# Probabilities times values in a latent attention: the stationary tile takes the values of two heads (128 columns) instead of one (64)

## The chip, the cores and the metric

The kernel runs on one core of one Trainium2 chip. Times are device microseconds of one execution. A profile of one execution shows the five engines: TensorE (PE its matmuls, PEld its weight loads), VectorE (DVE), ScalarE (ACT), GpSimd (POOL) and SyncE (SP, which issues the transfers here).

## The reference, cut to what matters

One step of a network with two layers, for 128 context tokens and 128 latent tokens. Each layer is a feed-forward part, a token mixer and another feed-forward part, with a normalisation behind each. The mixer has three branches: a convolution, a retention and an attention with low-rank queries and keys. The change is in the attention, in the product of probabilities and values:

```python
kv = (ckv_all @ lp['mla_w_ukv']).reshape(B, ckv_all.shape[1], MLA_HEADS, MLA_D_NOPE + MLA_D_V)
s = jnp.einsum('bqhd,bkhd->bhqk', qn, k_nope) + jnp.einsum('bqhd,bkd->bhqk', qr, k_rope)
p = jax.nn.softmax(s.astype(jnp.float32) * scale, axis=-1).astype(v.dtype)
out = jnp.einsum('bhqk,bkhd->bqhd', p, v)
mla_out = attn.reshape(B, T, MLA_HEADS * MLA_D_V) @ lp['mla_w_out']
```

There are 8 heads with 64 value columns each. A context token sees the 128 context keys; a latent token sees 128 cached keys and the 128 latent keys. So a head has three blocks of 128 x 128 probabilities.

## The kernel before, in words

Activations lie with features on partitions and the 256 tokens (128 context, 128 latent) along the free axis. The weights arrive as 458 units of up to 128 x 1024 values in the order in which they are used. ScalarE rounds a unit to a short format (`ring_hi`, line 692) and VectorE makes the rest (`ring_lo`, line 693), both in rings of five; a projection is then three matmuls per block of 128 features: high by high, high by low, low by high. The matmuls of a unit in the main chain are 24 for most projections; units with 512 moving columns have 12 or 18.

All instructions are first recorded in a `Program`. Its `order` (line 350) plays them through with modelled durations and due times, engine by engine, and each engine's instructions are then written in that order, which is fixed from then on. Main matmuls form one chain; side work (attention, retention, convolution taps, modulation products) is given slots with `sched` and is laid between the matmuls of the chain. The model of a matmul (`matmul`, line 454) depends on its moving columns, not on its stationary ones. A bank of the matmul memory counts as a whole when dependences are found (`region`, line 285). A side matmul on TensorE is ready only some time after what it needs (`PAD`, line 249).

The attention of a head has three steps. `att0` makes scores and probabilities: query times key, the maximum, the exponential with its sum, and the division. `att1` transposes the three blocks of probabilities on TensorE into bank C, and ScalarE copies them to `pt` (`ring_aa`). `att2` multiplies: the stationary operand is a block of values of this head, 128 keys x 64 columns out of `vm` (tile T6, shown as T in the profile), the moving operand the transposed probabilities of 128 tokens. The operands have 32-bit floats, and each such matmul leaves two loads and two matmuls in the trace. Even heads write partitions 0 to 63 of bank E and odd heads partitions 64 to 127, in the same 256 columns. After the odd head ScalarE copies the pair, rounded, into `catm` (tile CM), and VectorE subtracts that from the bank to make the low part; these are lines 1412 to 1415, recorded at lines 520 and 482. `catm` is read by the units `("mla", p)`, the first of which starts some 60 us after the last of these copies.

Of the kernel before, what the change touches and what calls it, by code (L numbers as in the profile page):

```python
# [8 lines left out]
F32 = mybir.dt.float32  # L9
# [3 lines left out]
AF = mybir.ActivationFunctionType  # L13
ALU = mybir.AluOpType
PSUM = bass.MemoryType.PSUM

P = 128
# [5 lines left out]
T = 256  # L23
# [541 lines left out]
class Trunk:  # L565
# [632 lines left out]
    def mixer(self, l):  # L1198
# [43 lines left out]
        for j in range(2):  # L1242
            ps = self.bank("C" if j == 0 else "B")
# [53 lines left out]
        ps = self.bank()  # L1297
# [29 lines left out]
        st = {}  # L1327
# [9 lines left out]
        for j in range(4):  # L1337
            ps = self.bank()
# [18 lines left out]
        vm = self.t("T6", [3, 512])  # L1357
# [14 lines left out]
        catm = self.t("CM", [4, 2, T], F32R)  # L1372
# [27 lines left out]

        def att2(h):
            pt = st.pop(("t", h))
            o = (h % 2) * 64
            if h % 2 == 0:
                st["o"] = self.bank("E")
            po = st["o"][o:o + 64]
            v = lambda b: vm[:, b, h * 64:(h + 1) * 64]
            nc.matmul(po[:, 0:TOK], v(0), pt[:, 0:TOK], start=True, stop=True)
            nc.matmul(po[:, TOK:T], v(1), pt[:, TOK:2 * TOK], start=True, stop=False)
            nc.matmul(po[:, TOK:T], v(2), pt[:, 2 * TOK:3 * TOK], start=False, stop=True)  # L1410
            if h % 2:
                ps = st["o"][:, 0:T]
                c = catm[:, h // 2, 0, :]
                self.act(c, ps, AF.Copy)
                self.tt(catm[:, h // 2, 1, :], ps, c.bitcast(F32), ALU.subtract)

        for h in range(MH):
            self.sched(h + 4, lambda h=h: att2(h))
# [291 lines left out]
        for f in range(KT):  # L1710
            ps = self.bank()
# [118 lines left out]
```

## Time and profile before

| what | value |
|---|---|
| time, median of 3 runs | 1413.1 us (1409.68 to 1414.0) |
| the profiled execution's own time | 1410.63 us |
| its span in the profile | 1408.9 us |
| PE busy | 1374.7 us (98%) |
| DVE busy | 1206.7 us (86%) |
| ACT busy | 765.8 us (54%) |
| read from the chip's memory | 321.28 MB, 230 GB/s over the span |
| mean granted TensorE clock | 0.995 of full speed |

How to read the rows below: a group row has the line, engine, operation, output<-inputs and shape, the count, the busy time and mean duration in ns of one, and the idle time of the engine just before them with what ended it. A matmul's `128*64` is the part of the array that it uses, rows by columns. The durations of matmuls overlap, since they are pipelined; what one costs is read from the start of one to the start of the next.

### The profile page before, as it was taken

How to read it: one execution, taken by the hardware profiler on the slowest of the kernel's cores; microseconds unless marked ns; L12 is line 12 of the kernel's file. 1: busy time of each engine (PE TensorE's matmuls, PEld its weight loads, DVE VectorE, ACT ScalarE, POOL GpSimd, SP SyncE). 2: the span in 40 equal slices, each digit the busy share in tenths (PEclk: the TensorE clock that was granted, in tenths of full speed). 3: DMA queues.
4: the chain of work that ended last, by engine and by line, in shares of the span. 5: the costliest groups of instructions: out<-in, count | busy, mean ns of one | idle time of the engine just before them, and what ended most of it. 6: DMA issues, size and time to landing. Idle time of an engine off the chain costs nothing.

```text
span 1408.9 us, 28827 instructions
## 1 busy us (share of the span) xinstructions
PE 1374.7 (98%) x11488; PEld 1309.0 (93%) x11488; DVE 1206.7 (86%) x2291; ACT 765.8 (54%) x1257; POOL 13.6 (1%) x28
## 2 busy tenths in 40 slices
PE   7999999999999999999999999999999999999996
PEld 5999998987999999999989999899788999899996
DVE  3899988998999988999989999799889998865565
ACT  4654447565554557444465454675555455754542
POOL 0000000000000000000000000000000000000000
PEclk9999999999999999999999999999999999999998
DMA  9998975753567767889658896655346767466561
GB/s 349 349 325 286 333 263 205 239 168 123 173 215 261 233 243 269 280 288 337 238 192 301 283 311 236 228 186 165 119 139 211 246 222 264 140 223 196 181 194 57
DMA packets 92166, 326.60 MB, mean 232 GB/s; under 512 B 10944, under 2 KB 11360, under 8 KB 91392
## 3 DMA queue, kind: packets, MB, share of 16 engines
q1 hardware_dynamic: 90432, 319.88, 66.5%
q0 software_dynamic: 1600, 4.88, 1.0%
q8 instruction: 90, 1.47, 0.4%
q14 instruction: 44, 0.36, 0.1%
HBM read 321.28 MB, written 3.44 MB: 230 GB/s over the span
## 4 chain that ended last, share of the span: by engine, by line
PE 91%; DVE 5%; DMA 3%; ACT 1%; issue 1%; SPq 0%; DVEq 0%; ACTq 0%
PE bankm L460 66%; PE bankE L460 18%; PE bankB L460 2%; PE bankA L460 2%; PE bankC L460 2%; DVE ring_lo L482 2%; DVE T L486 1%; DMA T<-in_ada 1%; DVE T L482 1%; DMA T<-in_x 1%; DMA ring_ada<-in_ada 0%; DMA ring_raw<-in_w 0%; PE bankC L473 0%; ACT ring_hi L520 0%; SPq L527 0%
## 5 line engine op out<-in xcount | busy, mean ns | idle before, releaser
L520 ACT ACTIVATE ring_hi<-ring_raw 128x1024 fp32r<-128x1024 f32 (+2 forms) x462 | 476.8, 1037 | 327.5 <-PE bankm L460 143.4
L482 DVE TENSOR_TENSOR ring_lo<-ring_raw,ring_hi 128x1024 fp32r<-128x1024 f32 (+2 forms) x462 | 546.0, 1192 | 81.7 <-ACT ring_hi L520 79.9
L460 PE MATMUL bankm<-ring_U,ring_hi 128*128 128x256 f32 x3296 | 588.4, 280 | 5.7 <-ACT ring_U L520 2.8
L460 PEld LDWEIGHTS bankm<-ring_U,ring_hi 128*128 128x128 f32 x3296 | 503.4, 189 | 12.4 <-ACT ring_U L520 3.7
L460 PE MATMUL bankm<-ring_U,ring_lo 128*128 128x256 f32 x1648 | 463.9, 281 | 0.2
L460 PEld LDWEIGHTS bankm<-ring_U,ring_lo 128*128 128x128 f32 x1648 | 310.8, 189 | 4.0 <-issue 2.3
L460 PE MATMUL bankm<-T,ring_hi 128*128 128x256 f32 x1464 | 255.1, 277 | 2.3 <-DVE T L482 2.3
L460 PEld LDWEIGHTS bankm<-T,ring_hi 128*128 128x128 f32 x1464 | 221.1, 188 | 3.4 <-ACT ring_hi L520 3.0
L460 PE MATMUL bankm<-T,ring_lo 128*128 128x256 f32 (+1 forms) x732 | 202.9, 277 | 0.0
L460 PE MATMUL bankE<-ring_U,ring_hi 128*128 128x256 f32 x832 | 146.8, 277 | 0.0
L460 PEld LDWEIGHTS bankm<-T,ring_lo 128*128 128x128 f32 x732 | 137.4, 188 | 0.0
L460 PEld LDWEIGHTS bankE<-ring_U,ring_hi 128*128 128x128 f32 x832 | 125.8, 188 | 0.4 <-issue 0.4
L486 DVE SCALAR_TENSOR_TENSOR T<-hp,cols,T 128x256 f32<-128x256 f32 x240 | 114.1, 481 | 3.8
L460 PE MATMUL bankE<-ring_U,ring_lo 128*128 128x256 f32 x416 | 115.3, 277 | 0.1
L460 PE MATMUL bankm<-ring_hi,ring_U 128*128 128x512 f32 x256 | 88.6, 414 | 0.0
L520 ACT ACTIVATE ring_tB<-bankm 128x256 f32<-128x256 f32 x84 | 31.7, 382 | 102.6 <-PE bankm L460 102.5
L460 PE MATMUL bankE<-T,ring_hi 128*128 128x256 f32 (+1 forms) x488 | 86.5, 279 | 0.0
L460 PEld LDWEIGHTS bankE<-ring_U,ring_lo 128*128 128x128 f32 x416 | 78.4, 188 | 0.3 <-DVE ring_lo L482 0.3
L486 DVE SCALAR_TENSOR_TENSOR ring_s<-ring_ada,ring_sg 128x1024 bf16<-128x1024 f32 (+2 forms) x68 | 74.3, 1093 | 2.5 <-DMA ring_ada<-in_ada 2.4
L460 PEld LDWEIGHTS bankE<-T,ring_hi 128*128 128x128 f32 x488 | 74.1, 188 | 1.0 <-DVE T L482 0.8
L486 DVE SCALAR_TENSOR_TENSOR ring_ada<-ring_ada,ring_sg 128x1024 f32<-128x1024 f32 (+2 forms) x68 | 73.8, 1092 | 0.1
L460 PE MATMUL bankE<-T,ring_lo 128*128 128x256 f32 (+1 forms) x244 | 68.1, 279 | 0.0
(263 smaller groups left out, 1594.0 us busy)
## 6 DMA issues: line engine op xcount, KB each, us to landing
ring_raw<-in_w SPq DMA_DIRECT2D x422, 512.0 KB, 4.4
ring_ada<-in_ada SPq DMA_DIRECT2D x107, 512.0 KB, 5.2
ring_raw<-in_w SPq DMA_DIRECT2D x32, 384.0 KB, 4.0
T<-in_ada SPq DMA_DIRECT2D x17, 512.0 KB, 7.7
ring_aa<-in_ada SPq DMA_DIRECT2D x10, 512.0 KB, 6.6
CM<-in_ada SPq DMA_DIRECT2D x6, 512.0 KB, 6.9
ring_sg<-in_crow SPq DMA_DIRECT2D x3, 1024.0 KB, 5.8
ring_raw<-in_w SPq DMA_DIRECT2D x8, 256.0 KB, 7.5
```

Of the source, the lines that this page charges most:

```text
L460: self.prog.add("PE", dur, lambda: self.nc.tensor.matmul(self.real(out), self.real(lhsT), self.real(rhs), start=start, stop=stop), [lhsT, ...
L482: self.dve(out, [in0, in1], lambda: self.nc.vector.tensor_tensor(out=self.real(out), in0=self.real(in0), in1=self.real(in1), op=op))
L486: self.dve(out, [in0, scalar, in1], lambda: self.nc.vector.scalar_tensor_tensor(out=self.real(out), in0=self.real(in0), scalar=self.real(s ...
L520: self.prog.add("ACT", dur, lambda: self.nc.scalar.activation(self.real(out), self.real(in_), func, **{k: self.real(v) for k, v in kw.item ...
```

## The change

The stationary operand becomes the values of both heads of a pair, 128 columns. Each head writes all 128 partitions, into its own half of bank E (columns 0 to 255 for the even head, 256 to 511 for the odd one). Of the even head's half only partitions 0 to 63 are of use, of the odd head's half partitions 64 to 127; the other rows are the products with the other head's values and are not read. The copy and the subtraction behind the odd head are made once for each half, on 64 partitions each.

```diff
         def att2(h):
             pt = st.pop(("t", h))
-            o = (h % 2) * 64
-            if h % 2 == 0:
+            e, pair = h % 2, h // 2
+            if e == 0:
                 st["o"] = self.bank("E")
-            po = st["o"][o:o + 64]
-            v = lambda b: vm[:, b, h * 64:(h + 1) * 64]
+            po = st["o"][:, e * T:(e + 1) * T]
+            v = lambda b: vm[:, b, pair * P:(pair + 1) * P]
             nc.matmul(po[:, 0:TOK], v(0), pt[:, 0:TOK], start=True, stop=True)
             nc.matmul(po[:, TOK:T], v(1), pt[:, TOK:2 * TOK], start=True, stop=False)
             nc.matmul(po[:, TOK:T], v(2), pt[:, 2 * TOK:3 * TOK], start=False, stop=True)
-            if h % 2:
-                ps = st["o"][:, 0:T]
-                c = catm[:, h // 2, 0, :]
-                self.act(c, ps, AF.Copy)
-                self.tt(catm[:, h // 2, 1, :], ps, c.bitcast(F32), ALU.subtract)
+            if e:
+                for a in range(2):
+                    rows = slice(a * 64, a * 64 + 64)
+                    ps = st["o"][rows, a * T:(a + 1) * T]
+                    c = catm[rows, pair, 0, :]
+                    self.act(c, ps, AF.Copy)
+                    self.tt(catm[rows, pair, 1, :], ps, c.bitcast(F32), ALU.subtract)
```

## Rows read from the trace of the kernel before

**Rows 1.** The page: busy us and share per engine; the last chain by engine.
```profile
PE 1374.7 (98%) x11488; PEld 1309.0 (93%) x11488; DVE 1206.7 (86%) x2291; ACT 765.8 (54%) x1257; POOL 13.6 (1%) x28
...
PE 91%; DVE 5%; DMA 3%; ACT 1%; issue 1%; SPq 0%; DVEq 0%; ACTq 0%
```

**Rows 2.** Groups of weight loads by form, whole span.
```profile
L460 PEld LDWEIGHTS bankE<-ring_aa,T 128*64 128x64 f32 x96 | 9.2, 134 | 12.0 <-issue 9.0 <-DVE ring_mx L502 0.7 <-DVE T L486 0.5
...
L460 PEld LDWEIGHTS bankA<-T 128*128 128x128 f32 x32 | 5.3, 189 | 0.3
```

**Rows 3.** Timeline of TensorE's matmuls: start us, us, engine, line, what, count.
```profile
307.90 0.63 PE L460 MATMUL bankm<-ring_hi,ring_U 128*128 128x512 f32 x2
308.45 0.43 PE L460 MATMUL bankE<-ring_aa,T 128*64 128x128 f32 x2
308.82 0.50 PE L460 MATMUL bankm<-ring_lo,ring_U 128*128 128x512 f32 x1
309.16 0.63 PE L460 MATMUL bankm<-ring_hi,ring_U 128*128 128x512 f32 x2
309.63 0.38 PE L460 MATMUL bankA<-T,T 128*128 128x128 f32 x2
309.84 0.27 PE L473 MATMUL bankC<-const,ring_aa 128*128 128x128 f32 x1
310.05 0.43 PE L460 MATMUL bankE<-ring_aa,T 128*64 128x128 f32 x2
310.41 0.50 PE L460 MATMUL bankm<-ring_lo,ring_U 128*128 128x512 f32 x1
310.74 0.63 PE L460 MATMUL bankm<-ring_hi,ring_U 128*128 128x512 f32 x2
...
311.44 0.27 PE L473 MATMUL bankC<-const,ring_aa 128*128 128x128 f32 x1
311.55 0.60 PE L460 MATMUL bankA<-T,T 128*128 128x256 f32 x2
...
314.05 0.43 PE L460 MATMUL bankE<-ring_aa,T 128*64 128x128 f32 x2
```

**Rows 4.** Timeline of the weight loads, same stretch; idle before and its end in brackets.
```profile
308.45 0.19 PEld L460 LDWEIGHTS bankE<-ring_aa,T 128*64 128x64 f32 x2 [0.36 <-issue]
308.82 0.19 PEld L460 LDWEIGHTS bankm<-ring_lo,ring_U 128*128 128x128 f32 x1 [0.17 <-issue]
...
309.40 0.42 PEld L460 LDWEIGHTS bankA<-T,T 128*128 128x128 f32 x2
```

**Rows 5.** Instructions of bank E: count, ns min/median/max, first and last start.
```profile
L520 ACT ACTIVATE CM<-bankE x8: 367/378/385, 310.9 to 1030.9; 128x256 fp32r<-128x256 f32 x8
L482 DVE TENSOR_TENSOR CM<-bankE,CM x8: 417/424/426, 311.8 to 1031.3; 128x256 fp32r<-128x256 f32 x8
```

**Rows 6.** Groups of ScalarE by form, whole span.
```profile
L520 ACT ACTIVATE T<-bankm 64x384 f32<-64x384 f32 x6 | 2.9, 487 | 6.0 <-PE bankm L460 6.0
```

**Rows 7.** Timeline of VectorE, 310 to 315 us.
```profile
311.83 0.42 DVE L482 TENSOR_TENSOR CM<-bankE,CM 128x256 fp32r<-128x256 f32 x1
```

**Rows 8.** Timeline of TensorE's matmuls, 411 to 413.5 us.
```profile
412.50 0.40 PE L460 MATMUL bankm<-ring_U,ring_hi 128*128 128x256 f32 x2
```

**Rows 9.** Timeline of VectorE, 380 to 416 us.
```profile
408.44 1.22 DVE L482 TENSOR_TENSOR ring_lo<-ring_raw,ring_hi 128x1024 fp32r<-128x1024 f32 x1
```

**Rows 10.** Stretches: us, busy of each engine, clock, transfers' share, GB/s.
```profile
301.00:346.00 45.00, 45.00 (x246) 32.45 (x245) 37.05 (x80) 23.29 (x54) 0.00 (x0) 1.00 0.39 127
346.00:410.00 64.00, 64.00 (x396) 57.41 (x395) 58.10 (x142) 35.97 (x62) 3.81 (x7) 1.00 0.53 172
410.00:440.00 30.00, 30.00 (x266) 29.46 (x266) 29.76 (x51) 13.97 (x18) 0.00 (x0) 1.00 0.85 278
```

**Rows 11.** TensorE's waits, whole span: us in total, times, longest.
```profile
PE bankm L460 <- ACT ring_hi L520: 2.1, 1, 2.1
```

## The prediction

> **What bounds the kernel now.** I read the page's shares and its chain first. TensorE is busy 98% of the span, the chain that ended last is 91% TensorE, and VectorE is the only other engine near full [rows 1]. So a TensorE microsecond saved is worth up to one microsecond, as long as VectorE can follow.
>
> Then the changed instructions. The 96 weight loads of the probabilities-times-values matmuls (two records a matmul: 48 matmuls, 24 a layer) have 64 columns, take 134 ns, and had 12.0 us of idle weight-load time right before them; a 128-column load takes 189 ns [rows 2]. That idle time is odd in a stage where nothing is missing, so I read the order of TensorE's instructions there [rows 3]. A 512-column matmul of the main chain starts 0.235 us after the one before (309.16 to 309.63 holds two). From 307.90 to 309.16 stand three of these and one 64-column matmul: 1.26 - 3 x 0.235 = 0.555 us for it. From 309.84 to 310.74 stand a transpose (0.11, from 311.44 to 311.55), one main matmul and again one 64-column matmul: 0.90 - 0.11 - 0.235 = 0.555. The query-times-key matmul at 309.63 has the same shape but 128 stationary columns: 0.21 us to the next start. I take 0.23, with 0.02 on top for what may start late behind it; so a visit at 64 columns costs 0.33 us more than one at 128.
>
> The loads show how it arises [rows 4]: the load for 64 columns starts 0.36 us after the load engine went idle, together with its matmul, and the main load behind it 0.17 us late, each put down to "issue"; the two loads of the 128-column matmul start at 309.40, ahead of their matmuls at 309.63. So a change of the tile's width, either way, keeps the next load from running ahead.
>
> No two of these matmuls stand side by side: 1.6 us and other work lie between 308.45 and 310.05 [rows 3], and so it is for all of them.
>
> [...]
>
> **The change, part by part.**
> *Matmuls.* 48 before, 48 after, with the same moving columns and two records each; width 128 throughout. Removed 48 x 0.555, added 48 x 0.23: 26.6 - 11.0 = 15.6 us less on TensorE, 7.8 us a layer, spread over the 44 us in which they stand. Bounds: with 0.21 for the 128-column matmul 16.6 us; at the other end the loads never run ahead (first rival), 5.3 us slower than now. I take 15.6, since the query-times-key matmul is the same instruction in the same stage.
>
> *Copies out.* Each pair of heads has one ScalarE copy (378 ns) and one VectorE subtraction (424 ns) of 128 x 256 [rows 5]; after it has two of each on 64 rows. A ScalarE copy of 64 x 384 takes 487 ns [rows 6], so rows don't make it cheaper and columns count: bounds 0.33 (487 x 256/384) to 0.38 us. I take the full price: 8 pairs x 0.38 = 3.0 us on ScalarE, 8 x 0.42 = 3.4 us on VectorE, 1.7 a layer. ScalarE is half idle. VectorE's share is weighed with the next step.
>
> *Hand-over of the bank.* The next pair's first matmul waits until both subtractions have read bank E. Now the first pair's subtraction ends at 312.25 [rows 7] and the next pair's first matmul starts at 314.05 [rows 3]: 1.8 us of room, against 0.80 us more (0.38 + 0.42). Three hand-overs a layer. Behind that matmul the whole main chain is queued, so a late one costs its delay one for one; the order of the instructions counts on a dependence, with a pad. TensorE comes there sooner than now, though, by up to the 0.33 of each matmul passed. Bounds 0 to 0.5 us each; I take 0.1, and 0.6 us for six.
>
> *What is late next: VectorE.* A main unit (24 matmuls) can't start before VectorE has written its low parts. Counting splits and matmuls in order (24 a projection unit, 12 or 18 for the others), slack in the attention stretch is 10 to 16 us. The smallest behind it is at the unit that starts at 412.50 [rows 8]: its low parts are written from 408.44 to 409.66 [rows 9], 2.85 us before. If TensorE arrives 7.8 us sooner, VectorE has to come 7.8 - 2.85 = 5.0 us sooner there, and carries 1.7 us more: 6.7 us. Its idle time is 45 - 37.05 = 7.95 us from 301 to 346 and 64 - 58.10 = 5.9 from 346 to 410; from 410 to 440 it has 0.24 left [rows 10]. So 6.7 of 13.85 us of idle time must go. Much of that idle time is waiting for TensorE's and ScalarE's results of the same stage, which come sooner too; some is the gap between small dependent instructions and stays. Cost at best 0; if none of it goes, 6.7 us a layer. I take 0.6 us a layer, 1.2 in both. Elsewhere slack is 4 us and more, and the weights keep coming: the transfers are busy 0.39 of the stretch from 301 to 346 [rows 10].
>
> **Sum.** 15.6 - 0.6 - 1.2 = 13.8 us less. The profiled execution took 1410.6 us (span 1408.9 and 1.7 around it): 1396.8. That execution lies 2.5 us under the median of the three runs; the same step from the median gives 1399.3. I forecast 1399.
>
> **Rivals.**
> 1. *The loads stay exposed (slower).* The late start may come not from the width but from the operands: load and matmul start together at 308.45 [rows 3, 4], as they would behind a wait for the transposed probabilities that ScalarE copies. Then the 0.555 us stay, and each load grows by 189 - 134 = 55 ns in the open: 96 x 0.055 = 5.3 us slower, 1415.9. It decides as soon as a 128-column matmul here costs over 0.555 us. Against it: 308.45 and 310.05 are the second and the last matmul of their head, wait for nothing new and pay the same, and the main load behind pays 0.17 [rows 4], though its operands are old. [...] Chance 0.05.
> 2. *VectorE becomes the bound.* None of its idle time goes. Then a layer gains only the slack less the new work, 2.85 - 1.7 = 1.15 us, 2.3 in both: 1408.3. For it: VectorE is full from 410 to 440. Against it: it is 10 us ahead and more where the gain arises, limited there by free buffers and by TensorE's results. A middle case (half of the idle time needed goes) costs 3.4 us a layer: 1410.6 - 15.6 + 0.6 + 6.7 = 1402.3. Chance of the whole 0.06, of the middle 0.15.
> 3. *The written order changes.* The planner lays out all engines' instructions by modelled times; four more copies and subtractions a layer can shuffle later stages. A main unit that waited for its split shows 2.1 us once [rows 11]; once in each of six stages would be 12.6 us: 1396.8 + 12.6 = 1409.4. For it: units with little slack at the start of each stage. Against it: the planner holds the matmul's duration the same, and the new work is 1.7 us a layer. It can as well gain. Chance 0.06.
>
> **How the numbers follow.** Forecast 0.68 (gain of 10 to 17 us), middle case 0.15, VectorE bound 0.06, order 0.06, slower 0.05. The range: low end 1409.7 (the fastest run) - 16.6 = 1393; the high end takes in the middle case and reaches to VectorE bound, 1409. What a measurement of this kernel can tell is 0.3%, 4.2 us: faster is below 1408.9. Forecast and middle case are faster, and part of the other two: 0.87. Within 0.3%: 0.08. Slower: 0.05.
>
> **What would show it.** The group of 96 matmuls into bank E reads 128*128, its loads take 189 ns, and the idle time of 12.0 us before them is gone; TensorE's starts around one of them are 0.11 us apart, and the load behind runs ahead. The stretch from the first to the last of them shrinks from 44 us to about 36. ScalarE and VectorE each show 16 instructions on CM of 64 x 256 where there were 8, at 0.38 and 0.42. A VectorE wait in front of main matmuls near the old 412 would be rival 2; an idle weight load of 0.2 to 0.4 us still before each of the 128-column matmuls would be rival 1, and the forecast would then be wrong.

## The result, and the profile after

| | before | changed |
|---|---|---|
| time, median | 1412.25 us (1409.68 to 1414.0, 4 runs) | 1396.46 us (1394.1 to 1397.4, 4 runs) |
| profiled execution | 1410.63 us | 1396.16 us |
| span | 1408.9 us | 1394.4 us |

The ratio is 0.9887, 95% interval 0.9867 to 0.9908: 15.8 us faster by the medians, where 13.8 were forecast (1399, range 1393 to 1409).

The page of the changed kernel, busy time by engine and the chain by engine; it answers to [rows 1]:

```profile
PE 1359.7 (98%) x11488; PEld 1312.2 (94%) x11488; DVE 1207.8 (87%) x2299; ACT 769.5 (55%) x1265; POOL 13.6 (1%) x28
...
PE 87%; DVE 7%; DMA 3%; ACT 2%; issue 1%; SPq 0%; DVEq 0%; ACTq 0%
```

As many matmuls and loads as before, 15.0 us less TensorE time, 3.2 us *more* load time, and 8 instructions more on ScalarE and VectorE each. The changed loads, from the groups of weight loads by form, against the first of [rows 2]:

```profile
L460 PEld LDWEIGHTS bankE<-ring_aa,T 128*128 128x128 f32 x96 | 15.9, 189 | 2.3
```

Each load is 55 ns longer, and the 12.0 us of idle time before them are 2.3. The timeline of the matmuls and, below it, of the loads at the same work as [rows 3, 4] (start, us, engine, line, what, count):

```profile
306.85 0.62 PE L460 MATMUL bankm<-ring_hi,ring_U 128*128 128x512 f32 x2
307.30 0.38 PE L460 MATMUL bankE<-ring_aa,T 128*128 128x128 f32 x2
307.44 0.48 PE L460 MATMUL bankm<-ring_lo,ring_U 128*128 128x512 f32 x1
307.76 0.62 PE L460 MATMUL bankm<-ring_hi,ring_U 128*128 128x512 f32 x2
308.22 0.38 PE L460 MATMUL bankA<-T,T 128*128 128x128 f32 x2
```

```profile
307.08 0.42 PEld L460 LDWEIGHTS bankE<-ring_aa,T 128*128 128x128 f32 x2
307.42 0.19 PEld L460 LDWEIGHTS bankm<-ring_lo,ring_U 128*128 128x128 f32 x1
```

The loads start at 307.08, ahead of their matmuls at 307.30, and no bracket stands behind them. From 306.85 to 307.76 lie three main matmuls and the changed one: 0.91 - 3 x 0.23 = 0.22 us, where it was 0.555. From the first to the last of these matmuls a layer now takes 36.7 us, where it took 43.6.

Where the time went, stage by stage. I counted units of the main chain in order, as in the prediction, and took the start of each unit's first matmul. The attention stretch is from the start of the first value unit to the start of the first gate unit: 299.41 to 350.99 before, 299.70 to 343.12 after.

| stretch, us | before | changed |
|---|---|---|
| main chain starts at | 16.70 | 17.18 |
| from there to the attention stretch, layer 1 | 282.70 | 282.52 |
| attention stretch, layer 1 | 51.58 | 43.42 |
| attention stretch, layer 2 | 51.58 | 43.42 |
| first eight units of the last feed-forward part | 22.30 | 23.83 |

Each attention stretch is 8.16 us shorter, 16.3 in both. All other stages agree within 0.1 us, but for the start (0.5 lost, 0.2 regained) and the last row, which loses 1.5. That loss is the clock. The stretches around the start of those units (us, busy time by engine, granted clock, transfers' share, GB/s), before and then changed:

```profile
1213.00:1219.00 6.00, 5.12 (x42) 4.71 (x41) 6.00 (x19) 5.98 (x16) 0.00 (x0) 1.00 0.02 4
```

```profile
1197.00:1203.00 6.00, 5.12 (x29) 4.75 (x28) 6.00 (x19) 5.98 (x16) 0.00 (x0) 0.72 0.01 3
```

The same six microseconds of work: before at a granted clock of 1.00, after at a mean of 0.72, with 29 matmuls done in place of 42. What TensorE did ahead of it was the same, the end of the normalisation (6.85 of 8 us busy in both). Both traces show such a drop at the start of another stage too, a mean of 0.79 over 716 to 724 us before and over 708 to 716 us after; the one at 1197 us stands in the changed kernel's alone. Why it comes in one execution and not in the next, no run here shows.

### The profile page after: what moved, and what is told of

Read it like the earlier page. It is cut to its first block, busy times and chain, and to the rows that moved or that the text cites. A ratio compares the mean times of both kernels' runs of the same rounds, so it can differ in the third digit from the quotient of the medians.

```text
span 1394.4 us, 28854 instructions
## 1 busy us (share of the span) xinstructions
PE 1359.7 (98%) x11488; PEld 1312.2 (94%) x11488; DVE 1207.8 (87%) x2299; ACT 769.5 (55%) x1265; POOL 13.6 (1%) x28
## 4 chain that ended last, share of the span: by engine, by line
PE 87%; DVE 7%; DMA 3%; ACT 2%; issue 1%; SPq 0%; DVEq 0%; ACTq 0%
PE bankm L460 63%; PE bankE L460 17%; DVE ring_lo L482 3%; PE bankA L460 2%; DVE T L486 2%; PE bankB L460 2%; PE bankC L460 2%; DMA T<-in_ada 1%; ACT ring_hi L520 1%; DMA ring_raw<-in_w 1%; DVE T L482 1%; DMA T<-in_x 1%; DMA ring_ada<-in_ada 0%; PE bankC L473 0%; DVE ring_w L482 0%
## 5 line engine op out<-in xcount | busy, mean ns | idle before, releaser
L460 PEld LDWEIGHTS bankm<-ring_U,ring_hi 128*128 128x128 f32 x3296 | 504.5, 189 | 11.3 <-ACT ring_U L520 4.0
```

The lines of the kernel that those rows point to most:

```text
L460: self.prog.add("PE", dur, lambda: self.nc.tensor.matmul(self.real(out), self.real(lhsT), self.real(rhs), start=start, stop=stop), [lhsT, ...
```

## The experiments

Theory A: the price belongs to the change of width between neighbouring matmuls. Rivals: B, the new layout of the bank brings the gain; C, VectorE's new work costs; D, each narrow load is exposed whatever stands beside it; E, any tile that is not full pays. Times are medians; the ratio is to the kernel before on the same chip. Three chips were used, and the kernel before had a median of 1412.57 us on the first (e1, e5, e3, e4), 1411.46 on the second (e3a, e4s, e2, e6) and 1413.09 on the third (e7, e8).

| kernel | us | ratio (95%) | attention stretch, layers 1 and 2 |
|---|---|---|---|
| e1_halves_64col | 1412.01 | 0.9996 (0.9984 to 1.0008) | 51.47, 51.47 |
| e5_96col | 1396.08 | 0.9884 (0.9869 to 0.9898) | 43.45, 43.45 |
| e3_head_in_one_visit | 1402.9 | 0.9932 (0.9919 to 0.9946) | 45.91, 45.90 |
| e3a_128_head_in_one_visit | 1394.94 | 0.9878 (0.9857 to 0.9899) | 43.33, 43.31 |
| e4_pair_in_one_visit | 1393.18 | 0.9864 (0.9851 to 0.9878) | 41.80, 41.80 |
| e4s_heads_in_turn | 1395.49 | 0.9884 (0.9862 to 0.9907) | 42.91, 42.91 |
| e2_one_copy | 1394.91 | 0.9876 (0.9855 to 0.9896) | 43.36, 43.36 |
| e6_copies_twice | 1401.47 | 0.9922 (0.9905 to 0.994) | 45.27, 45.26 |
| e7_changed_again | 1395.69 | 0.9875 (0.9859 to 0.9892) | 43.42, 43.42 |
| e8_pair_again | 1394.32 | 0.9867 (0.9845 to 0.9888) | 41.80, 41.80 |

The stretch repeats to 0.02 us between layers and runs, so it tells apart what the times alone could not.

**e1: the copies and the halves without the width.**

```diff
-            po = st["o"][:, e * T:(e + 1) * T]
-            v = lambda b: vm[:, b, pair * P:(pair + 1) * P]
+            po = st["o"][e * 64:e * 64 + 64, e * T:(e + 1) * T]
+            v = lambda b: vm[:, b, h * 64:(h + 1) * 64]
```

> The other half of the change alone: each head in its own half of bank E and two copies and two subtractions a pair, but the stationary tile stays one head's 64 columns. Theory A (the price is the change between 64- and 128-column tiles): nothing gained, 1411 to 1413 us. Rival B (the layout of the bank, its dependences, brings the gain): 1397 to 1400. Rival C (VectorE's 3.4 us more are on the path): 1414 to 1416.

The time is as before within the interval, and each stretch is only 0.11 us shorter. The load engine, by form, still stands idle before these loads:

```profile
L460 PEld LDWEIGHTS bankE<-ring_aa,T 128*64 128x64 f32 x96 | 9.2, 134 | 12.1 <-issue 8.3 <-ACT ring_aa L520 0.7 <-DVE ring_aa L492 0.7
```

B and C fall: the layout brings nothing, and the second copy and the second subtraction of a pair cost nothing that can be measured.

**e5: 96 columns.**

```diff
-            po = st["o"][:, e * T:(e + 1) * T]
-            v = lambda b: vm[:, b, pair * P:(pair + 1) * P]
+            po = st["o"][0:96, e * T:(e + 1) * T]
+            v = lambda b: vm[:, b, pair * P:pair * P + 96]
```

> The changed kernel with 96 stationary columns instead of 128 (the second head's half bank gets only 96 rows, so part of the attention's output is wrong). Theory A in the form that what counts is the array tile in use (128*128 for more than 64 columns): like the changed kernel, 1395 to 1398. Rival E (any tile that is not full pays): 1410 to 1413.

The whole gain is there. Its loads by form:

```profile
L460 PEld LDWEIGHTS bankE<-ring_aa,T 128*96 128x96 f32 x96 | 14.1, 162 | 2.9
```

This tile is not full and does not pay, so E falls. The price is there at 64 columns and gone at 96 (51.47 and 43.45 us of stretch); widths between were not run. The trace lists the tile as 128*96, so that it counts as 128*128 is not shown; what is shown is that its stretch is that of 128 columns, 43.42.

**e3 and e3a: a head's three matmuls as one item of the order,** with 64 columns and with 128.

```diff
+    def group(self, items):
+        def fn():
+            for out, lhsT, rhs, start, stop in items:
+                r = self.nc.tensor.matmul(self.real(out), self.real(lhsT), self.real(rhs), start=start, stop=stop)
+            return r
+        dur = sum(2 * max(107, _n(x[2]) / 1.2) for x in items)
+        self.prog.add("PE", dur, fn, [y for x in items for y in x[1:3]], [x[0] for x in items])
...
-            nc.matmul(po[:, 0:TOK], v(0), pt[:, 0:TOK], start=True, stop=True)
...
+            nc.group([(po[:, 0:TOK], v(0), pt[:, 0:TOK], True, True),
...
```

> The kernel before, with the three 64-column matmuls of a head laid behind one another as one item of the order: 16 visits to the narrow tile instead of 48. Theory A (price per change of width): a visit costs 0.555 + 4 x 0.11 = 0.99 us instead of 3 x 0.555 = 1.67, 16 x 0.68 = 10.8 us less, about 1401 us. Rival D (every 64-column load is exposed, whatever stands beside it): no change, 1410 to 1413.

> The changed kernel (128 columns) with the three matmuls of a head laid behind one another. Theory A: nothing is left that depends on the number of visits, so the attention stretch and the time stay, 1395 to 1398. If a visit of side work costs something whatever its width: 10 us less as with 64 columns, about 1386.

With 64 columns each stretch is 5.7 us shorter than before, 11.3 in both, where 10.8 were worked out; the median is 9.7 lower. Loads and a visit, from the groups by form and the timeline of the matmuls of e3:

```profile
L475 PEld LDWEIGHTS bankE<-ring_aa,T 128*64 128x64 f32 x96 | 10.0, 136 | 4.2 <-issue 3.9 <-DVE T L495 0.3
```

```profile
301.57 0.63 PE L460 MATMUL bankm<-ring_hi,ring_U 128*128 128x512 f32 x2
302.12 0.87 PE L475 MATMUL bankE<-ring_aa,T 128*64 128x128 f32 x6
302.92 0.50 PE L460 MATMUL bankm<-ring_lo,ring_U 128*128 128x512 f32 x1
```

A visit is one stay in the narrow tile. One visit of six records takes 0.80 us, where three separate visits took 3 x 0.37, and a third of the idle load time is left, with as many narrow loads. D falls. With 128 columns the same regrouping moves the stretch by 0.1 us: nothing there depends on the number of visits. With the same grouping, 64 columns cost 45.91 - 43.33 = 2.58 us a layer more than 128, 0.32 us for each of 8 visits; for each of the 24 visits of a single matmul it is 8.16/24 = 0.34. So the price goes by the visit and not by the matmul. What holds the load back at a change of width, no run here shows; the rows show only that it starts together with its matmul.

**e4 and e4s: both heads of a pair in one visit,** alternating or in turn, 64 columns each.

```diff
+            for b, c0, start, stop in ((0, 0, True, True), (1, TOK, True, False), (2, TOK, False, True)):
+                for e in range(2):
+                    po = st["o"][e * 64:e * 64 + 64]
+                    g = h - 1 + e
+                    items.append((po[:, c0:c0 + TOK], vm[:, b, g * 64:(g + 1) * 64], st["t", g][:, b * TOK:(b + 1) * TOK],
+                                  start, stop))
+            nc.group(items)
...
-        for h in range(MH):
-            self.sched(h + 4, lambda h=h: att2(h))
+        for h in range(1, MH, 2):
+            self.sched(h + 3, lambda h=h: att2(h))
```

e4s exchanges the two loops over `b` and `e`.

> The kernel before, with all six 64-column matmuls of a pair of heads in one visit, the heads alternating: 8 visits. Theory A without overlap of the two heads: a visit costs 0.555 + 10 x 0.11 = 1.66 us instead of 3.33, 8 x 1.67 = 13.4 us less, about 1399. [...] Rival D: no change, 1410 to 1413.

> As the kernel with a pair of heads in one visit (8 visits of six 64-column matmuls), but the three matmuls of the even head first and then those of the odd head, instead of alternating. If the gain of the alternating order came from fewer visits alone: the same as there, about 1393. [...]

Timeline of the matmuls of e4, one visit, and then of e4s, one visit:

```profile
304.06 0.38 PE L460 MATMUL bankB<-T,T 128*128 128x128 f32 x2
304.37 0.88 PE L475 MATMUL bankE<-ring_aa,T 128*64 128x128 f32 x12
305.18 0.33 PE L482 MATMUL bankC<-const,ring_aa 128*128 128x128 f32 x1
```

```profile
301.66 1.14 PE L475 MATMUL bankE<-ring_aa,T 128*64 128x128 f32 x12
302.74 0.33 PE L482 MATMUL bankC<-const,ring_aa 128*128 128x128 f32 x1
```

Alternating, twelve records take 0.81 us, as long as six of one head in e3: the records of the two heads start 7 ns apart and each head steps at 0.109 us, so the two halves of the array do work beside each other. In the order of before, the two heads never stood side by side, as the prediction read from its rows. The two stretches of e4 are 19.6 us shorter than before, where 13.4 were worked out for heads that do not overlap. In turn a visit takes 1.07 us: the second head's first matmul starts 0.275 us after the first head's and runs beside it from there. I had expected no overlap in turn, so a visit of 1.66 us, as in the first case of e4; that miss is 0.59 us a visit. By the visits, alternating is worth 8 x 0.26 = 2.1 us over in turn, and by the stretches 2.2, so the gain of e4 does not come from fewer visits alone. The stretch of e4 is 1.62 us shorter than the changed kernel's, that of e4s 0.51 (42.91 against 43.42).

e7 and e8 are the changed kernel and e4 once more, with no edit, side by side on one chip.

> The changed kernel once more, beside the kernel with a pair of heads in one visit: 1395 to 1397.5 us.

> The kernel with 64 columns and a pair of heads in one visit, alternating, on the same chip as the changed kernel. Its attention stretch (start of the first value unit to start of the first gate unit) was 41.80 us a layer against 43.42 in the changed kernel: 3.2 us less in both layers, 1392 to 1394.5. If that gain is given back elsewhere: 1395 to 1397.

On that chip the two medians are 1395.69 and 1394.32, each in its range, with ratios whose intervals overlap. The 3.2 us of the two stretches are there in both pairs of traces, but runs of one kernel differ by as much (1394.1 to 1397.4 for the changed one), and clock drops weigh as much: e4's profiled execution (1396.09 us) has them at three stage starts, near 711, 898 and 956 us (granted clock 0.79 over 8 us each), where e8's (1391.37 us, the same kernel) has 1.00, and e8's has one near 1194 us that e4's has not; over the whole span the mean is 0.990 in e4 and 0.992 in e8. e4 is the version to take, by its traces; the times do not settle it.

**e2 and e6: fewer and more copies.** e2 takes one copy and one subtraction of 128 rows from the even head's half:

```diff
-                for a in range(2):
-                    rows = slice(a * 64, a * 64 + 64)
-                    ps = st["o"][rows, a * T:(a + 1) * T]
-                    c = catm[rows, pair, 0, :]
-                    self.act(c, ps, AF.Copy)
-                    self.tt(catm[rows, pair, 1, :], ps, c.bitcast(F32), ALU.subtract)
+                ps = st["o"][:, 0:T]
+                c = catm[:, pair, 0, :]
+                self.act(c, ps, AF.Copy)
+                self.tt(catm[:, pair, 1, :], ps, c.bitcast(F32), ALU.subtract)
```

e6 makes each of the four twice:

```diff
-                    self.act(c, ps, AF.Copy)
-                    self.tt(catm[rows, pair, 1, :], ps, c.bitcast(F32), ALU.subtract)
+                    for _ in range(2):
+                        self.act(c, ps, AF.Copy)
+                        self.tt(catm[rows, pair, 1, :], ps, c.bitcast(F32), ALU.subtract)
```

> The changed kernel with one copy and one subtraction of 128 rows from the even head's half, as before the change; the odd head's result is left out. If the doubled copies cost what the prediction took for VectorE and the hand-over (1.8 us): 1394 to 1395. If VectorE's slack hides them: like the changed kernel, 1395.5 to 1397.

> The changed kernel with every copy and subtraction made twice: 32 more instructions, 6.7 us more VectorE and 6.0 us more ScalarE work. Covered by slack: 0 to 1 us over the changed kernel, 1396 to 1397.5. VectorE is the bound behind the attention (2.85 us of slack a layer): up to 3.4 us a layer, 1400 to 1403.

Without the second copy the stretch is 0.06 us shorter a layer: the added work of the change is covered. The median of e2, 1394.91, lies by itself in the range that I had given for a cost of 1.8 us; but its five runs spread from 1390.3 to 1396.4 and the kernel before was 0.8 us faster on this chip than in the result, so the stretch decides. Doubled, the work is not covered, and each stretch grows by 1.85 us, 3.7 of the 5.0 by which the profiled execution is longer than the changed kernel's. The time is the one that I had tied to VectorE's slack behind the attention, but the place is another: there (from the first gate unit to the unit at the old 412) e6 takes 61.73 us and the changed kernel 61.49. TensorE waits at the hand-over of bank E; from the timeline of e6 (idle time before and its end in brackets):

```profile
320.86 0.87 DVE L482 TENSOR_TENSOR CM<-bankE,CM 64x256 fp32r<-64x256 f32 x2
321.82 0.78 ACT L520 ACTIVATE CM<-bankE 64x256 fp32r<-64x256 f32 x2 [0.42 <-DVE CM L482]
322.64 0.88 DVE L482 TENSOR_TENSOR CM<-bankE,CM 64x256 fp32r<-64x256 f32 x2 [0.39 <-ACT CM L520]
323.57 0.30 PEld L460 LDWEIGHTS bankE<-ring_aa,T 128*128 128x128 f32 x2 [0.85 <-DVE CM L482]
```

The repeated copy also overwrites what the subtraction reads, so the two engines take turns, and e6 lengthens the chain by more than the doubled work. TensorE's waits of this kind in the first stretch sum to 1.3 us of the 1.85; where the rest comes from stays open.

## Why the prediction was right

*The price of the narrow tile.* 48 x 0.325 = 15.6 us were forecast, 16.3 measured in the two stretches, 0.34 us a matmul. The 128-column matmul costs about 0.22 us in the changed kernel, near the bare reading of [rows 3], 0.21; most of the 0.02 on top was not needed. Rival 1, exposed loads, is out: the loads run ahead, and those of 307.08 start while the main matmuls of 306.85 run (to 307.47). What lets them do so, no run here shows.

*The copies.* 16 of each, as forecast, at the full price; they answer to [rows 5] (count, ns min/median/max, first and last start):

```profile
L520 ACT ACTIVATE CM<-bankE x16: 364/378/381, 309.5 to 1016.0; 64x256 fp32r<-64x256 f32 x16
L482 DVE TENSOR_TENSOR CM<-bankE,CM x16: 407/422/428, 310.4 to 1017.7; 64x256 fp32r<-64x256 f32 x16
```

*The hand-over.* 0.6 us were taken, nothing came. VectorE, against [rows 7], and the next pair's first matmul:

```profile
310.45 0.85 DVE L482 TENSOR_TENSOR CM<-bankE,CM 64x256 fp32r<-64x256 f32 x2
```

```profile
312.43 0.38 PE L460 MATMUL bankE<-ring_aa,T 128*128 128x128 f32 x2
```

The second subtraction ends at 311.30, and 1.13 us of room are left of 1.8. This first hand-over, the one that the prediction read, is the widest of the six: the others of layer 1 have 0.73 and 0.41 us, those of layer 2 1.02, 0.62 and 0.30 (before, all six had 1.7 to 1.8). TensorE does come sooner at each, as the prediction said, and it was close. VectorE and TensorE at the narrowest:

```profile
1007.14 0.86 DVE L482 TENSOR_TENSOR CM<-bankE,CM 64x256 fp32r<-64x256 f32 x2
```

```profile
1008.30 0.38 PE L460 MATMUL bankE<-ring_aa,T 128*128 128x128 f32 x2
```

In e6 TensorE starts 0.05 to 0.06 us after the last subtraction at all six, so there the hand-over sets its start: this room was the right thing to look at.

*VectorE.* 1.2 us were taken, nothing came. The unit at the old 412.50 and its low parts, against [rows 8, 9]:

```profile
404.62 0.40 PE L460 MATMUL bankm<-ring_U,ring_hi 128*128 128x256 f32 x2
```

```profile
400.58 1.22 DVE L482 TENSOR_TENSOR ring_lo<-ring_raw,ring_hi 128x1024 fp32r<-128x1024 f32 x1
```

TensorE is 7.88 us earlier and VectorE 7.86, with its new work done besides: the slack is 2.82 us, where it was 2.85. Idle time did go, as argued: of the 13.85 us of [rows 10] 6.0 are left (from 301 to 402), and by the waits below most of what went was waiting for the other engines' results. VectorE's waits from 300 us to this unit, changed kernel (us in total, times, longest):

```profile
DVE ring_s L486 <- ACT ring_aa L520: 0.7, 1, 0.7
DVE ring_aa L482 <- PE bankB L460: 0.4, 1, 0.4
DVE ring_bs L505 <- PE bankB L460: 0.3, 1, 0.3
DVE CM L482 <- ACT CM L520: 0.2, 1, 0.2
```

That is 1.6 us, where nine kinds of waits had made 9.5 before. Rival 2 is out, its middle case too. Rival 3 as well: the order of TensorE's instructions did change in places, and no stage but the attention moved by more than the start and the clock do.

*The sum.* The two costs of 1.8 us that did not come and the 0.7 by which the first term was too small make the profiled difference 2.5 us larger than forecast; the start and the clock drop took 1.8 of that back, 14.5 against 13.8. That the profiled difference came so near is thus in part luck: two errors of the sum one way, and a late start and a clock drop, of which the forecast had nothing, the other. By the medians it is 15.8.

## What to carry to other kernels

Look for idle weight-load time with no wait behind it: here (32-bit floats, 128 moving columns, granted clock 1.00) a 64-column matmul between full ones pays about 0.34 us a visit, for the way in and the way out together. Widening the stationary tile to 96 or 128 columns removed it here (43.45 and 43.42 us of stretch, 51.58 before) even where half of the result is thrown away, since the extra columns cost nothing in the stream (within a visit the records start 0.11 us apart with 64 columns and with 128); laying narrow matmuls of different column tiles side by side in one visit removed most of it and used both halves (41.80 us in e4). Before costing an engine's idle time as lost slack, see what it waits for: here VectorE's waits on the stage that got faster shrank with it, from 9.5 to 1.6 us.

## What I had not expected of the hardware

A load takes 134 ns for 64 columns, 162 for 96 and 189 for 128, but in the price of the change of width 96 columns stand with 128, not between: 43.45 and 43.42 us of stretch, against 51.47 for 64. And two 64-column tiles overlap without strict alternation: in e4s the second head starts 0.275 us after the first, and a visit takes 1.07 us.
